# Projections between attention steps, handed out eight products at a time

## The chip, the core and the metric

The kernel runs on one core of a Trainium2 chip. The metric is the device time of one execution in microseconds (us); smaller is better. Five engines work side by side, each through its own queue in order: TensorE (PE in the profile; its weight loads are listed apart as PEld), VectorE (DVE), ScalarE (ACT), GpSimd (POOL) and SyncE (SP), which issues the DMAs. TensorE writes its results into eight PSUM banks of 128 x 512 float32; VectorE and ScalarE read them from there.

## What is computed

One layer of a hybrid decoder, for 1024 tokens of width 1024, in float32:

```python
h = rms_norm(x, g_attn)
z = h @ w_in                       # queries, keys, values, gates of both branches
o_fox = fox_attention(...)         # 8 heads, causal, with a forgetting bias
o_nsa = nsa_attention(...)         # 8 heads, 2 key groups: compressed, selected and window keys
merged = sigmoid(g_a) * (o_fox @ w_br_fox) + sigmoid(g_b) * (o_nsa @ w_br_nsa)
x = x + merged @ w_out
h = rms_norm(x, g_mlp)
x = x + square(relu(h @ w_ff1)) @ w_ff2
return rms_norm(x, g_final)
```

To keep float32 accuracy, an operand is split into an upper part (rounded, "hi") and a lower part (the rest, "lo"), and a product is summed from three combinations: lo x hi, hi x lo and hi x hi.

## The kernel before

The normalised input stays in on-chip memory, transposed and split, as four tiles: `hTh` and `hTl`, one pair for each half of 512 tokens. A **projection** (`proj`) makes 128 output rows for one half: three combinations, each with 8 slices of the inner dimension, are 24 products of 512 columns that add up in one PSUM bank. Its weights are fetched, split by ScalarE (line 206) and VectorE (line 207), and asked for through `wget`. When the last product is issued, `done` takes the bank out and splits the result again.

**Attention** is cut into units: one head and 256 queries in the first stage (FoX), two heads and 256 queries in the second (NSA). A unit has score steps (products of queries and keys; VectorE adds the bias and takes the minimum, line 825; ScalarE takes the exponential, line 838; GpSimd scales, line 841) and then chunks. A **chunk** turns up to four 128 x 128 blocks of the weighted scores (`ptf`, `ptn`: transposes on TensorE, line 160, into one of two PSUM banks of tag "T"), splits the turned tile (`PTf`, `PTn`: a CAST on ScalarE, then a TENSOR_TENSOR on VectorE, both line 864) and multiplies it with the values into `accs`. This is a handover: TensorE to ScalarE to VectorE and back to TensorE. The same two instructions free the T bank, so the transposes of the chunk after next wait for them too.

**What sets the order.** The projections that later units need (and the gates `g`) are written as a list of steps, the feed, each with a cost. `attend` walks through the attention's steps and adds up what the feed is owed by then; when half of the next step's cost is owed, that step is emitted. Attention steps carry a higher priority, and a feed step may not move more than 5000 ns of cost ahead of its place. From this a scheduler with its own time model writes each engine's final instruction order; it may cut a step of several products and put attention instructions between them. Before the change a feed step is four products of one projection: six steps for each half, of `4 * MM` cost.

Not all projections go through the feed: those of the first head pair run before the attention with 256 columns each (`parts=2`). The products of the branches (`brf`, `brn`) have their own steps of six.

The lines that matter: `proj` (316), `wget` (218), `pv` (894: two chunks of transposes run ahead of the first product), `attend` (1114), and the pools with two T banks, three score banks and two projection banks (143 to 154).

Of the kernel before, what the change touches and what calls it, by code (L numbers as in the profile page):

```python
# [120 lines left out]
MM = 216.0  # L121
# [3 lines left out]
class Kernel:  # L125
# [190 lines left out]
    def proj(self, st, n, half, name, done, psf=None, parts=1):  # L316


        nc = self.nc
        box = {}  # L320
        w_ = H // parts

        def part(q, i):
            hi, lo = self.wget(n, name not in self.LATE or half > 0 or i >= 4)
            if q == 0 and i == 0:
                box["ps"] = (psf or self.psP)(f"{name}_{half}")
            c = slice(q * w_, q * w_ + w_)
            hh, hl = self.hT[half]

            ops = ((hi, hh), (hi, hl), (lo, hh)) if parts > 1 else ((lo, hh), (hi, hl), (hi, hh))  # L330
            mm = [(w, h, k) for w, h in ops for k in range(8)]
            for m in range(4 * i, 4 * i + 4):
                w, h, k = mm[m]
                self.mm(box["ps"][:, c], w[:, k, :], h[:, k, c], start=m == 0, stop=m == 23)
            if q == parts - 1 and i == 5:
                done(box["ps"])

        for q in range(parts):
            s = st[q] if parts > 1 else st
            for i in range(6):  # L340
                s.add(4 * MM / parts, lambda q=q, i=i: part(q, i), n)

    def proj_half(self, st, n, half, name, done, psf=None):
        if len(st) == 4:
# [1705 lines left out]
```

## Time and profile before

| | |
|---|---|
| median of 3 runs | 1576.82 us (1576.37 to 1577.49) |
| the profiled execution's own time | 1578.03 us |
| its span, first to last instruction | 1576.3 us |
| instructions | 23267 |
| input and first head pair | 0 to about 100 us |
| FoX units with their feed | about 100 to 345 us |
| NSA units with their feed | about 345 to 830 us |
| merge and MLP | about 830 to 1576 us |

A row of the profile names the source line, engine and operation, then output<-inputs, shapes and a count; behind a bar stand busy time and the mean duration. In a timeline a row begins with its start and length in us, and "[0.72 <-DVE ...]" is the time that the engine stood idle before it and who ended the wait. A row of PEld is a weight load: it runs ahead while the product before it is still flowing, so an idle time shown there is the most that the products themselves can have waited.

### The profile page before, as it was taken

To read this page: it belongs to the slowest core of one execution; us is meant where nothing else is said; L and a number is where in the kernel's file an instruction comes from. 1 tells how busy PE (TensorE), PEld (TensorE's weight loads), DVE (VectorE), ACT (ScalarE), POOL (GpSimd) and SP (SyncE) were. 2 spreads that over 40 slices of the span, in tenths; PEclk is the share of its full clock that TensorE was granted. 3 is DMA by queue.
4 is the path that set the end of the run, shared out by engine and by line. 5 is a ranking of instruction groups with operands and counts; after the bars stand their busy time and mean duration, and the time that the engine had idled before them with its cause. 6 is when DMAs were issued, how large, how long until landed. Compare 5 with 4: busy or idle time off the path is not lost.

```text
span 1576.3 us, 23267 instructions
## 1 busy us (share of the span) xinstructions
PE 1559.3 (99%) x7920; PEld 1314.5 (83%) x7920; DVE 1103.1 (70%) x2450; ACT 861.0 (55%) x1620; POOL 365.5 (23%) x433
## 2 busy tenths in 40 slices
PE   8999999999999999999999999999999999999998
PEld 7888888888888888888888887888888888888886
DVE  7667768757666677648658389665556599777877
ACT  6666666646565676558533267555555644333335
POOL 1133323213333333336310000433333100000002
PEclk9999999999999999999999999999999999999999
DMA  6321211342121112214458542554444696545312
GB/s 192 77 59 49 65 49 56 96 110 65 58 81 57 44 54 74 66 64 135 149 169 314 179 161 87 194 169 155 158 147 147 222 325 215 160 146 167 114 54 107
DMA packets 165951, 196.66 MB, mean 125 GB/s; under 512 B 21497, under 2 KB 101433, under 8 KB 165825
## 3 DMA queue, kind: packets, MB, share of 16 engines
q1 hardware_dynamic: 165832, 195.18, 38.5%
q8 instruction: 63, 1.03, 0.3%
q14 instruction: 56, 0.45, 0.1%
HBM read 139.99 MB, written 55.15 MB: 124 GB/s over the span
## 4 chain that ended last, share of the span: by engine, by line
PE 90%; DVE 4%; DMA 2%; ACT 2%; SPq 1%; issue 1%; POOL 0%; DVEq 0%; ACTq 0%
PE g L157 11%; PE fX L157 11%; PE oX L157 10%; PE accs L157 8%; PE fZ L157 6%; PE oZ L157 5%; PE wo L157 4%; PE ptn L160 3%; PE nq L157 3%; PE brn L157 3%; PE fk L157 3%; PE fv L157 3%; PE fq L157 3%; PE fW L157 2%; PE oW L157 2%; PE sn L157 2%
## 5 line engine op out<-in xcount | busy, mean ns | idle before, releaser
L157 PE MATMUL oX<-to,so 128*128 128x512 f32 x672 | 154.6, 389 | 0.0
L157 PEld LDWEIGHTS oX<-to,so 128*128 128x128 f32 x672 | 126.2, 188 | 26.2
L864 DVE TENSOR_TENSOR PTn<-ptn,PTn 128x512 fp32r<-128x512 f32 (+1 forms) x136 | 90.7, 673 | 70.3 <-ACT PTn L864 69.6
L1873 ACT CAST to<-w 128x1024 fp32r<-128x1024 f32 x48 | 48.2, 1051 | 145.0 <-PE accs L157 54.0
L864 ACT CAST PTn<-ptn 128x512 fp32r<-128x512 f32 (+1 forms) x136 | 76.4, 571 | 64.1 <-PE ptn L160 56.8
L157 PE MATMUL fX<-ht,w1h 128*128 128x512 f32 x384 | 94.9, 389 | 0.6 <-DVE ht L1579 0.6
L1711 POOL TENSOR_TENSOR ss<-w 128x512 f32<-128x512 f32 x14 | 22.4, 1601 | 308.6 <-DMA w<-in_w_ff_dram 188.5
L157 PE MATMUL accs<-PTn,Vnv 128*128 128x512 f32 (+1 forms) x304 | 91.8, 392 | 0.5 <-DVE PTn L864 0.5
L157 PEld LDWEIGHTS fX<-ht,w1h 128*128 128x128 f32 x384 | 72.0, 188 | 15.9 <-DVE ht L1579 1.0
L841 POOL TENSOR_SCALAR pf<-pf,rdf 128x896 f32<-128x896 f32 (+3 forms) x64 | 51.2, 807 | 142.0 <-DVE rdf L840 116.4
L1991 POOL TENSOR_TENSOR z<-x,gf 128x512 f32<-128x512 f32 x8 | 11.0, 1400 | 306.3 <-DVE x L1922 303.9
L157 PE MATMUL oZ<-to,so 128*128 128x512 f32 x336 | 77.6, 389 | 0.0
L157 PE MATMUL g<-hTh,wh_g 128*128 128x512 f32 (+1 forms) x288 | 76.5, 390 | 1.1 <-ACT hTh L311 1.1
L1701 DVE TENSOR_TENSOR w1l<-w,w1h 128x1024 fp32r<-128x1024 f32 (+1 forms) x32 | 34.6, 1081 | 59.7 <-ACT w1h L1700 59.7
L157 PE MATMUL g<-hTl,wh_g 128*128 128x512 f32 (+1 forms) x288 | 75.3, 384 | 0.0
L157 PEld LDWEIGHTS oZ<-to,so 128*128 128x128 f32 x336 | 63.1, 188 | 13.1
L157 PE MATMUL g<-hTh,wl_g 128*128 128x512 f32 x256 | 71.2, 397 | 0.0
L1874 DVE TENSOR_TENSOR so<-hr,so 128x1024 fp32r<-128x1024 f32 x56 | 68.0, 1237 | 1.2 <-ACT so L1873 1.2
L1873 ACT CAST so<-hr 128x1024 fp32r<-128x1024 f32 x56 | 56.7, 1049 | 19.7 <-DMA hr<-hid_d 19.7
L838 ACT ACTIVATE pf<-pf,mf 128x896 f32<-128x896 f32 (+3 forms) x64 | 49.7, 777 | 24.0 <-DVE mf L825 21.5
L1874 DVE TENSOR_TENSOR to<-w,to 128x1024 fp32r<-128x1024 f32 x48 | 56.7, 1221 | 7.7 <-ACT to L1873 7.3
L157 PEld LDWEIGHTS g<-hTh,wh_g 128*128 128x128 f32 x288 | 51.9, 192 | 10.7 <-ACT hTh L311 1.8
(513 smaller groups left out, 4248.7 us busy)
## 6 DMA issues: line engine op xcount, KB each, us to landing
w<-in_w_ff_dram SPq DMA_DIRECT2D x62, 512.0 KB, 4.6
hr<-hid_d SPq DMA_DIRECT2D x56, 512.0 KB, 4.2
wr_wo<-in_w_out_dram SPq DMA_DIRECT2D x20, 512.0 KB, 3.9
x<-in_x_dram SPq DMA_DIRECT2D x16, 512.0 KB, 8.9
wr_g<-in_w_in_dram SPq DMA_DIRECT2D x16, 512.0 KB, 3.8
hid_d<-h22s SPq DMA_DIRECT2D x32, 256.0 KB, 2.1
hid_d<-s2s SPq DMA_DIRECT2D x32, 256.0 KB, 2.0
hid_d<-s3h SPq DMA_DIRECT2D x32, 256.0 KB, 2.3
```

The lines of the kernel that those rows point to most:

```text
L157: self.last = self.nc.tensor.matmul(*a, **k)
L160: self.last = self.nc.tensor.transpose(*a, **k)
L838: nc.scalar.activation(p, p, AF.Exp, bias=nm, scale=-1.0, accum_out=den)
L841: self.scaled = nc.gpsimd.tensor_scalar(p, p, r, 1.0 if gate is None else gate, op0=OP.mult, op1=OP.mult).ins
L864: two = nc.scalar.copy(th, src).ins, nc.vector.tensor_sub(tl, src, th.bitcast(F32)).ins
L1701: nc.vector.tensor_sub(lo, src, hi.bitcast(F32))
L1711: e.tensor_add(p[:, 4:8], b[:, 0:4], b[:, 4:8])
L1873: nc.scalar.copy(o[:, 0, s], src)
L1874: nc.vector.tensor_sub(o[:, 1, s], src, o[:, 0, s].bitcast(F32))
L1991: nc.gpsimd.tensor_mul(y[:, c], x[:, c], gf[:, c])
```

## The change

A feed step of a projection with 512 columns now holds eight products, all of one combination of upper and lower parts, where it held four. There are three such steps for a half, each with twice the cost. Projections with `parts=2` keep steps of four. Nothing else in the program is touched: the same 24 products in the same sequence, the same weights, the same banks.

```diff
@@ proj
         w_ = H // parts
+        size = 4 if parts > 1 else 8
 
         def part(q, i):
-            hi, lo = self.wget(n, name not in self.LATE or half > 0 or i >= 4)
+            hi, lo = self.wget(n, name not in self.LATE or half > 0 or i * size >= 16)
...
             mm = [(w, h, k) for w, h in ops for k in range(8)]
-            for m in range(4 * i, 4 * i + 4):
+            for m in range(size * i, size * i + size):
                 w, h, k = mm[m]
                 self.mm(box["ps"][:, c], w[:, k, :], h[:, k, c], start=m == 0, stop=m == 23)
-            if q == parts - 1 and i == 5:
+            if q == parts - 1 and m == 23:
                 done(box["ps"])
 
         for q in range(parts):
             s = st[q] if parts > 1 else st
-            for i in range(6):
-                s.add(4 * MM / parts, lambda q=q, i=i: part(q, i), n)
+            for i in range(24 // size):
+                s.add(size * MM / parts, lambda q=q, i=i: part(q, i), n)
```

What it does to the order of TensorE is seen at three places. In the rows, `ptf_3_0` is chunk 0 of FoX unit 3, and `ptn_3_8` chunk 8 of NSA unit 3; the last number only makes a name unique.

First place, FoX stage, the keys' compression projection `kc` beside unit 3 of a head (TensorE). Before:

```order
L160 MATMUL ptf_3_0_2890<-idn,pf_7_2829 128x128
L160 MATMUL ptf_3_1_2909<-idn,pf_7_2829 128x128
L160 MATMUL ptf_3_1_2909<-idn,pf_6_2784 128x128
L160 MATMUL ptf_3_1_2909<-idn,pf_7_2829 128x128
L157 MATMUL kc_3113<-hTl_83,wh_kc 128x512 x4
L160 MATMUL ptf_3_2_2917<-idn,pf_6_2784 128x128
L160 MATMUL ptf_3_2_2917<-idn,pf_7_2829 128x128
```

After:

```order
L160 MATMUL ptf_3_0_2890<-idn,pf_7_2829 128x128
L160 MATMUL ptf_3_1_2905<-idn,pf_7_2829 128x128
L160 MATMUL ptf_3_1_2905<-idn,pf_6_2788 128x128
L160 MATMUL ptf_3_1_2905<-idn,pf_7_2829 128x128
L157 MATMUL accs<-PTf_3_2889,Vfv_2130 128x256
L160 MATMUL ptf_3_2_2921<-idn,pf_6_2788 128x128
L157 MATMUL accs<-PTf_3_2889,Vfv_2130 128x256
```

Each piece begins with the last transpose of chunk 0. The four products of `kc` behind the transposes of chunk 1 are gone from here; they follow further down as part of a block of eight. The products with `PTf_3_2889`, the turned tile of chunk 0, now come right behind the transposes; before, `kc` and the transposes of chunk 2 stood ahead of them.

Second place, NSA stage, the second group's values `nv` beside unit 3 (TensorE). Before:

```order
L157 MATMUL accs<-PTn_3_6357,Vnv_4291 128x512 x2
L157 MATMUL nv_1_6506<-hTl_85,wh_nv_6161 128x512 x4
L160 MATMUL ptn_3_9_6453<-idn,wn_6_5927 128x128
L160 MATMUL ptn_3_9_6453<-idn,wn_7_6002 128x128
L160 MATMUL ptn_3_9_6453<-idn,wn_6_6062 128x128
L160 MATMUL ptn_3_9_6453<-idn,wn_7_6124 128x128
L157 MATMUL accs<-PTn_3_6390,Vnv_4291 128x512 x2
L157 MATMUL nv_1_6506<-hTh_84,wh_nv_6161 128x512 x8
L160 MATMUL ptn_3_10_6482<-idn,wn_6_5927 128x128
L160 MATMUL ptn_3_10_6482<-idn,wn_7_6002 128x128
L160 MATMUL ptn_3_10_6482<-idn,wn_6_6062 128x128
L160 MATMUL ptn_3_10_6482<-idn,wn_7_6124 128x128
```

After:

```order
L160 MATMUL ptn_3_8_6424<-idn,wn_6_5927 128x128
L157 MATMUL accs<-PTn_3_6357,Vnv_4291 128x512
L160 MATMUL ptn_3_8_6424<-idn,wn_7_6010 128x128
L160 MATMUL ptn_3_8_6424<-idn,wn_6_6062 128x128
L160 MATMUL ptn_3_8_6424<-idn,wn_7_6124 128x128
L157 MATMUL accs<-PTn_3_6390,Vnv_4291 128x512
L160 MATMUL ptn_3_9_6457<-idn,wn_6_5927 128x128
L160 MATMUL ptn_3_9_6457<-idn,wn_7_6010 128x128
L157 MATMUL accs<-PTn_3_6390,Vnv_4291 128x512
L160 MATMUL ptn_3_9_6457<-idn,wn_6_6062 128x128
L160 MATMUL ptn_3_9_6457<-idn,wn_7_6124 128x128
L160 MATMUL ptn_3_10_6478<-idn,wn_6_5927 128x128
```

Before, blocks of four and eight products of `nv` separate the chunks. Now chunks 8, 9 and 10 stand one behind the other, and the next block of eight comes only after chunk 10.

Third place, NSA stage, the second group's keys `nk` beside unit 1 (TensorE). Before:

```order
L157 MATMUL nk_0_6882<-hTl_83,wh_nk_6613 128x512 x8
L157 MATMUL nk_0_6882<-hTh_82,wh_nk_6613 128x512 x8
L160 MATMUL ptn_1_6_6849<-idn,c_10_6181 128x128
L160 MATMUL ptn_1_6_6849<-idn,c_11_6259 128x128
L157 MATMUL accs<-PTn_1_6743,Vnv_4291 128x512 x2
L157 MATMUL nk_1_7044<-hTh_84,wl_nk_6614 128x512 x4
L157 MATMUL accs<-PTn_1_6807,Vnv_4291 128x512
L160 MATMUL ptn_1_7_6888<-idn,pn_3_6262 128x128
L157 MATMUL accs<-PTn_1_6807,Vnv_4291 128x512
L160 MATMUL ptn_1_7_6888<-idn,pn_3_6417 128x128
L160 MATMUL ptn_1_7_6888<-idn,wn_3_6306 128x128
L160 MATMUL ptn_1_7_6888<-idn,wn_3_6468 128x128
```

After:

```order
L157 MATMUL nk_0_6890<-hTh_82,wh_nk_6619 128x512 x8
L160 MATMUL ptn_1_5_6804<-idn,wn_2_6234 128x128
L160 MATMUL ptn_1_5_6804<-idn,wn_3_6310 128x128
L160 MATMUL ptn_1_5_6804<-idn,wn_2_6383 128x128
L160 MATMUL ptn_1_5_6804<-idn,wn_3_6468 128x128
L157 MATMUL accs<-PTn_1_6695,Vnv_4291 128x512 x2
L160 MATMUL ptn_1_6_6845<-idn,c_10_6181 128x128
L160 MATMUL ptn_1_6_6845<-idn,c_11_6267 128x128
L157 MATMUL accs<-PTn_1_6743,Vnv_4291 128x512 x2
L160 MATMUL ptn_1_7_6877<-idn,pn_3_6270 128x128
L160 MATMUL ptn_1_7_6877<-idn,pn_3_6421 128x128
L160 MATMUL ptn_1_7_6877<-idn,wn_3_6310 128x128
```

Chunk 5 has moved from ahead of `nk_0` (where the first piece does not reach) to behind it, and the four products of `nk_1` between chunks 6 and 7 have gone. On ScalarE the same place reads, before:

```order
L864 CAST PTn_1_6807<-ptn_1_5_6808 128x512
L838 ACTIVATE pn_5_6801,denn_5s<-pn_5_6801,mn_5_12_6820 128x768
L838 ACTIVATE wn_5_6846,denn_5w<-wn_5_6846,mn_5w_6867 128x640
L622 CAST ks_6928<-nk_0_6882 64x512
L623 CAST ks_6928<-nk_0_6882 64x512
L858 CAST PTn_1_6848<-ptn_1_6_6849 64x256
```

and after:

```order
L839 ACTIVATE pn_5_6801,denn_5s<-pn_5_6801,mn_5_12_6824 128x768
L839 ACTIVATE wn_5_6842,denn_5w<-wn_5_6842,mn_5w_6867 128x640
L623 CAST ks_6928<-nk_0_6890 64x512
L624 CAST ks_6928<-nk_0_6890 64x512
L865 CAST PTn_1_6803<-ptn_1_5_6804 128x512
L859 CAST PTn_1_6844<-ptn_1_6_6845 64x256
```

The cast of chunk 5's tile (`ptn_1_5`) stood ahead of the two casts of `nk_0`; now it stands behind them.

## The prediction

> **What bounds the kernel now.** I read the page's busy times first, then the chain of waits, then the busy times by stage, and last the list of who waits for whom, on TensorE's two rows, in the two attention stages that the change touches.
>
> ```profile
> span 1576.3 us, 23267 instructions
> ...
> PE 1559.3 (99%) x7920; PEld 1314.5 (83%) x7920; DVE 1103.1 (70%) x2450; ACT 861.0 (55%) x1620; POOL 365.5 (23%) x433
> ...
> PE 90%; DVE 4%; DMA 2%; ACT 2%; SPq 1%; issue 1%; POOL 0%; DVEq 0%; ACTq 0%
> ```
>
> TensorE is busy all the time and makes 90% of the chain that ended last. A change can win only by taking away waits of TensorE, and lose only by adding them. How many there are in the touched stages:
>
> ```profile
> core 0: us, PE busy (x) PEld busy (x) DVE busy (x) ACT busy (x) POOL busy (x), PEclk, DMA share, GB/s
> 0.00:100.00 100.00, 94.21 (x626) 82.71 (x627) 71.56 (x184) 65.88 (x126) 20.77 (x39) 0.98 0.45 122
> 100.00:345.00 245.00, 244.40 (x1452) 213.53 (x1451) 175.46 (x494) 148.67 (x304) 72.74 (x84) 1.00 0.24 68
> 345.00:830.00 485.00, 482.94 (x2556) 408.22 (x2555) 316.60 (x1089) 291.04 (x696) 169.39 (x246) 1.00 0.27 84
> ```
>
> Products stand still for 0.6 us in the FoX stage and 2.1 us in the NSA stage, but a product's shown end includes its way through the array, so short waits hide in it. The weight loads show more. FoX stage first, then NSA stage, with the sum, the number and the longest wait:
>
> ```profile
> PEld ptf L160 <- DVE PTf L864: 1.8, 4, 0.6
> ...
> PEld accs L157 <- DVE PTf L864: 0.4, 1, 0.4
> ...
> PEld accs L157 <- DVE PTn L864: 1.2, 3, 0.7
> PEld accs L157 <- DVE PTn L859: 1.1, 2, 0.9
> PEld sn L157 <- DVE mn L825: 0.8, 1, 0.8
> PEld ptn L160 <- DVE PTn L864: 0.6, 2, 0.4
> PEld sn_2w L157 <- DVE mn L825: 0.5, 1, 0.5
> ```
>
> With the small ones left out here (1.7 us in FoX, 1.0 us in NSA) these waits are 9.1 us in 730 us. That is the ceiling of any gain. Of these, 4.0 us (1.8 + 0.4 + 1.2 + 0.6) are at the handover of line 864: transposes, CAST, TENSOR_TENSOR, and then either the products with the turned tile or the next transposes into the same bank. So the question is what the new order does to these handovers.
>
> **The price of a handover and of what stands in it.** The place of `kc` in the old order shows one in full (timeline); the rows behind it, from the chain of waits, the timeline and the costliest groups, price the instructions of TensorE:
>
> ```profile
> 241.92 0.66 PE L160 MATMUL ptf<-idn,pf 128*128 128x128 f32 x4 [0.21 <-DVE PTf L864]
> ...
> 242.66 0.59 ACT L864 CAST PTf<-ptf 128x512 fp32r<-128x512 f32 x1 [1.04 <-PE ptf L160]
> ...
> 243.28 0.69 DVE L864 TENSOR_TENSOR PTf<-ptf,PTf 128x512 fp32r<-128x512 f32 x1 [0.83 <-ACT PTf L864]
> ...
> 244.03 0.19 PEld L157 LDWEIGHTS accs<-PTf,Vfv 128*128 128x128 f32 x1 [0.38 <-DVE PTf L864]
> ...
> 992.40 5.44 PE fX L157 x24
> ...
> 106.95 1.20 PE L157 MATMUL accs<-PTf,Vfv 128*128 128x256 f32 x8
> ...
> 533.58 0.60 PE L160 MATMUL ptn<-idn,wn 128*128 128x128 f32 x4
> ...
> L157 PE MATMUL oX<-to,so 128*128 128x512 f32 x672 | 154.6, 389 | 0.0
> ...
> 243.46 0.27 PE L160 MATMUL ptf<-idn,pf 128*128 128x128 f32 x1
> ...
> 243.49 0.36 PE L157 MATMUL accs<-PTf,Vfv 128*128 128x256 f32 x1
> ```
>
> The last of four transposes starts 0.27 us before their end at 242.58, at 242.31; the first product with the tile starts at 244.03. The handover costs 1.72 us from the start of the last transpose, with neither engine held up by other work. What TensorE issues in between covers it: a product of 512 columns takes 0.227 us (5.44 / 24), one of 256 columns 0.12 us ((1.20 - 0.36) / 7), a transpose 0.11 us ((0.60 - 0.27) / 3). The old order at this place has one transpose of chunk 0, three of chunk 1 and four products of `kc` before the bank is wanted again: 0.11 + 0.33 + 0.91 = 1.35 us, so 0.37 us of wait, and the row of the products shows 0.38. The price fits.
>
> **The change part by part.** The work is the same: 35 projections of two halves and 24 products, 1680 products in 210 steps instead of 420. No product, transpose, cast or DMA is added; I cost the work itself at nothing. What moves is where the products stand. In TensorE's order the rows of four products of these projections fall from 139 to 35, and those of eight rise from 72 to 108. A block of four covers 0.91 us of a handover and needs 0.8 us of other work beside it; a block of eight covers 1.82 us, more than it needs, but leaves the next gap empty. I went through the new order chunk by chunk, took the spacing from the last transpose to whoever needs the tile or its bank, and set it against 1.72 us:
>
> - `kc`, the first place: the products with `PTf_3_2889` come 0.11 + 0.33 = 0.44 us after the transpose, a wait of 1.28. The two waits of 0.37 there before are covered by it. **+0.54**.
> - The same unit one and two heads earlier (beside `fk`): one transpose, eight products of 256 and three transposes, 0.11 + 0.96 + 0.33 = 1.40, wait 0.32, twice. There was a block of four there before, and no wait. **+0.64**.
> - `nv`, the second place: chunk 6 has a spacing of 1.44 (wait 0.28); then chunk 10's transposes need the bank of chunk 8 with one transpose, two products of 512 and four transposes in between, 0.11 + 0.45 + 0.44 = 1.00 (wait 0.72). **+1.00**.
> - Beside gate 6 (`g_6`), chunk 5 after chunk 3: 0.11 + 0.23 + 0.45 + 0.44 = 1.23, wait 0.49. **+0.49**.
> - Beside gate 5 in the third pair, chunk 9 after chunk 7, again 1.00. **+0.72**.
>
> The third place, `nk`, needs ScalarE's queue. Before:
>
> ```profile
> 565.91 1.98 PE L157 MATMUL nk<-hTh,wh_nk 128*128 128x512 f32 x8
> ...
> 567.92 0.58 ACT L622 CAST ks<-nk 64x512 fp32r<-64x512 f32 x1 [0.84 <-PE nk L157]
> ...
> 568.52 0.58 ACT L623 CAST ks<-nk 64x512 fp32r<-64x512 f32 x1
> ...
> 569.13 0.68 DVE L624 TENSOR_TENSOR ks<-nk,ks 64x512 fp32r<-64x512 f32 x1 [1.78 <-ACT ks L623]
> ...
> 572.26 0.19 PEld L157 LDWEIGHTS accs<-PTn,vcmp 128*128 128x128 f32 x1 [0.92 <-DVE PTn L859]
> ```
>
> Now the cast of chunk 5 is queued behind the two casts of `nk_0`, and its subtraction behind that of `nk_0` on VectorE. From the end of `nk_0`'s last product the tile is ready after 0.03 + 1.18 + 0.03 + 0.68 + 0.69, about 2.6 us (two casts, then the two subtractions one after the other). TensorE wants chunk 5's bank for chunk 7 about 1.4 us after that end: ten instructions of 1.57 us, less the last product's way out of 0.16 us (0.389 - 0.227). The wait is about 1.2 us; the 0.92 us in the row above, 4 us further on, then falls away, as everything behind it is later. **+0.28**. If it stays, the place costs 0.9 more.
>
> One place gets better, beside the branch of FoX:
>
> ```profile
> 740.60 0.30 PEld L157 LDWEIGHTS sn_2w<-kw,Qnq 128*128 128x128 f32 x2 [0.49 <-DVE mn L825]
> ...
> 741.27 0.30 PEld L157 LDWEIGHTS sn<-ks,Qnq 128*128 128x128 f32 x2 [0.37 <-DVE mn_3w L825]
> ...
> 742.29 0.19 PEld L157 LDWEIGHTS accs<-PTn,Vnv 128*128 128x128 f32 x1 [0.72 <-DVE PTn L864]
> ```
>
> The two transposes that end chunk 0 have moved 0.68 us forward, so about 0.6 of the last wait goes; the scores moved back by 0.22 wait that much longer for VectorE. **-0.40**.
>
> The sum is 0.54 + 0.64 + 1.00 + 0.49 + 0.72 + 0.28 - 0.40 = 3.3 us, each place at the price of a handover with free queues. They are not always free. At `nv` the new order has a weight split directly ahead of chunk 6's cast, on both engines:
>
> ```profile
> L206 ACT CAST wh_g<-wr_g 128x1024 fp32r<-128x1024 f32 x16 | 16.7, 1042 | 0.0
> ...
> L207 DVE TENSOR_TENSOR wl_g<-wr_g,wh_g 128x1024 fp32r<-128x1024 f32 x16 | 19.9, 1243 | 4.6 <-ACT wh_g L206 4.4
> ```
>
> It is an instruction of 1.04 and 1.24 us, and a handover that comes during it waits half of one on average. I add 0.5 us for that, bounded by nothing below and by the longest wait of the old order, 0.92 us, at each of the seven places above, 6.4 us. So +3.8 us: 1581.8 for an execution like the profiled one (1578.0), and, as that one lies 1.2 us above the median of the runs shown (1576.8), **1580.6 us** against that median.
>
> **The rivals.**
>
> *The waits trade places, no change.* The 9.1 us hold some 5 us beside those counted above, and a TensorE that is held up at one place finds later tiles ready. If the new waits use up the old ones nearby, as at `nk`, the sum is about 0 and the time 1576.8. Speaking for it is the `nk` place. Against it, the other places that get worse have no old wait close behind.
>
> *Eight cover a handover, faster.* 1.82 us is more than 1.72, and 0.91 is not. Were there a block in each handover, the 4.0 us on line 864 would go: 1572.8. Against it stand the three places in the order, where the block comes once in two or three chunks. It decides the sign if the new order's handovers without a block are fewer than the old ones with half of one; I count more. [...] The trace shows no gain from longer batches alone: the eight of `nk` above take (1.98 - 0.389) / 7, again 0.227 us each.
>
> *The queues behind, much slower.* Chunks that come without projection work between them, one in 0.89 us (four transposes and two products), ask ScalarE for 0.59 and VectorE for 0.69 each time, on top of softmax and splits; VectorE is busy for 316.6 of 485 us in the NSA stage. If each of the seven places met a queue as long as the longest wait before, 6.4 us come on top: 1576.8 + 3.3 + 6.4 = 1586.5.
>
> *The clock drops.* More waits could cost TensorE its clock: 0.98 stands in the first 100 us, which hold its long waits, and 1.00 in both attention stages with 9.1 us of short ones. A loss of 0.02 in one stretch of 245 us is 4.9 us: with the sum 1585.5. [...]
>
> *The change does nothing,* because the scheduler cuts the steps again. It does cut some (64 rows of one product), but the counts of fours and eights show that most blocks stand.
>
> **How the numbers follow.** More handovers uncovered, +2 to +6 us: 56%. Traded, within 2 us: 22%. Queues, +6 to +12: 12%. Eight cover, -2 to -5: 7%. Clock: 3%. A measurement of this kernel can tell about 0.2%, 3.2 us, from no change. The forecast lies just above that, so a quarter of the first case counts as no change: slower 0.42 + 0.12 + 0.03 = 0.57; faster only where the fourth case goes beyond 3.2 us or so, 0.06; no change the rest, 0.37. The range for 8 in 10 runs from the traded case, 1576.6, to the queues' 1586.5; the forecast alone holds 1579 to 1583.
>
> **What would show it.** In the profile after: waits of PEld on line 864 (there line 865) of about 7 us in the two stages instead of 4.0, with one of 1.2 us or more at `kc` (near 241 us) and one at `nk` (near 568 us), and clocks of 1.00. The branches, merge and MLP behind 830 us should be the same but shifted. Wrong would be: these sums at 4 or less, or a loss that stands in other rows, such as weights' DMAs or scores.

## The result, and the profile after

The changed kernel takes 1588.09 us (median of 5 executions, 1587.08 to 1588.99) against 1576.72 us in the same session: a ratio of 1.0067, with a 95% interval of 1.0057 to 1.0078. It is **slower by 11.4 us (0.7%)** by the medians, 10.6 by the ratio. The prediction had the sign; the size is three times the 3.8 us that it gave, and lies above its range (1586.5).

The page of the profiled execution (1588.99 us), and TensorE by stage (start and end of the stretch, its length, then busy time and number of instructions of each engine, granted clock, DMA):

```profile
span 1587.3 us, 23244 instructions
...
PE 1563.8 (99%) x7920; PEld 1314.6 (83%) x7920; DVE 1104.3 (70%) x2450; ACT 861.7 (54%) x1620; POOL 363.0 (23%) x433
...
PE 91%; DVE 4%; ACT 2%; DMA 2%; issue 1%; SPq 1%; DVEq 0%; ACTq 0%
```

```profile
100.00:345.00 245.00, 240.13 (x1413) 209.03 (x1411) 171.55 (x492) 148.98 (x302) 71.79 (x81) 0.99 0.24 68
345.00:830.00 485.00, 479.45 (x2534) 403.66 (x2534) 316.87 (x1084) 288.72 (x691) 168.47 (x250) 1.00 0.27 82
```

The span grew by 11.0 us; PE stands still for 4.9 us of the FoX stretch (0.6 before) and 5.6 us of the NSA stretch (2.1 before), and in the FoX stage the clock is no longer 1.00. Who waits for whom, for weight loads, first from 100 to 345 us, then from 345 to 841 us (sum, number, longest):

```profile
PEld accs L157 <- DVE PTf L865: 2.3, 4, 1.4
PEld hT_kc L160 <- ACT PTf L865: 1.4, 1, 1.4
PEld hT_vc L160 <- DVE sg_vc L716: 1.3, 1, 1.3
...
PEld nq L157 <- DVE wl_nq L207: 0.9, 1, 0.9
```

```profile
PEld ptn L160 <- DVE PTn L865: 4.1, 4, 1.9
PEld accs L157 <- DVE PTn L865: 3.4, 6, 1.5
PEld sn L157 <- DVE mn L826: 0.8, 1, 0.8
PEld sn_2w L157 <- DVE mn L826: 0.7, 1, 0.7
```

The handover of line 864 (now 865) has 9.8 us of waits (2.3 + 4.1 + 3.4) instead of 4.0. Three rows are new in kind: `hT_kc`, `hT_vc` and `nq`. They belong to the compression of the keys and values, whose last steps (a sigmoid, two transposes `hT`) stand beside the end of the FoX stage, and to the first projection of the NSA stage.

For a finer account I took, for every instruction of TensorE, the time from its start to the next start, less the lower quartile of the same sequence of shapes (the instruction before, itself and the next) in the kernel before. From 100 to 840 us these **excess times** are 5.4 us (FoX) and 10.7 us (NSA) before, and 12.1 and 15.9 us after: 11.8 us more. The changed kernel leaves these stages 11.8 us later than the kernel before, and 0.9 of that is given back behind them, which leaves the 11.0 of the span. All figures called excess below are made so; products at a slow clock count in them. Behind 840 us the work is the same.

Two places show the kind of loss. The first lies between the two attention stages. Rows of the changed kernel's timeline, then of the kernel before at the same place:

```profile
322.81 1.22 DVE L207 TENSOR_TENSOR wl_w1vc<-wr_w1vc,wh_w1vc 128x1024 fp32r<-128x1024 f32 x1
...
324.05 0.37 SPq L187 DMA_DIRECT2D wr_nk<-in_w_in_dram  x1
...
330.51 1.05 ACT L206 CAST wh_nk<-wr_nk 128x1024 fp32r<-128x1024 f32 x1 [2.73 <-DMA wr_nk<-in_w_in_dram]
...
333.54 0.43 PE L160 MATMUL hT_vc<-idn,sg_vc 126*128 126x126 f32 x2 [1.06 <-DVE sg_vc L716]
...
334.67 3.53 PE L157 MATMUL nq<-hTh,wl_nq 128*128 128x512 f32 x8 [0.70 <-DVE wl_nq L207]
...
337.99 2.20 PE L157 MATMUL nq<-hTl,wh_nq 128*128 128x512 f32 x8
```

```profile
318.50 0.99 SPq L187 DMA_DIRECT2D wr_nk<-in_w_in_dram  x2
...
323.34 1.05 ACT L206 CAST wh_nk<-wr_nk 128x1024 fp32r<-128x1024 f32 x1 [0.46 <-DMA wr_nk<-in_w_in_dram]
...
329.71 2.11 PE L157 MATMUL nq<-hTh,wl_nq 128*128 128x512 f32 x8
```

Weights are loaded into two buffers. The DMA for `nk` goes out when the split of the compression's third weight tile has freed its buffer, at 324.05 instead of 318.50 us. ScalarE then stands 2.73 us for it with the sigmoid of `sg_vc` and the cast of `nq` queued behind, VectorE's instructions follow, and TensorE waits at `hT_vc` and at `nq`. Before, the same products started without a wait. Behind these waits eight products of `nq` take 3.32 us (334.67 to 337.99), 0.415 us each instead of 0.227. The stretches of the changed kernel around it:

```profile
332.00:335.00 3.00, 1.25 (x8) 0.74 (x7) 2.97 (x6) 2.40 (x4) 1.32 (x1) 1.00 0.32 67
335.00:339.00 4.00, 4.00 (x12) 3.14 (x11) 1.77 (x4) 1.04 (x1) 0.09 (x1) 0.58 1.14 281
```

The granted clock is 0.58 over 4 us, that is 1.7 us lost (0.42 x 4).

The second place is chunk 6 beside `nv`, for which the prediction had a wait of 0.28:

```profile
541.48 0.59 ACT L647 COPY vtnv<-nv 128x512 f32<-128x512 f32 x1 [3.00 <-PE nv L157]
...
541.96 1.05 ACT L206 CAST wh_nq<-wr_nq 128x1024 fp32r<-128x1024 f32 x1
...
542.90 1.07 ACT L865 CAST PTn<-ptn 128x512 fp32r<-128x512 f32 x2
...
543.04 1.22 DVE L207 TENSOR_TENSOR wl_nq<-wr_nq,wh_nq 128x1024 fp32r<-128x1024 f32 x1 [3.84 <-ACT wh_nq L206]
...
544.18 1.28 DVE L865 TENSOR_TENSOR PTn<-ptn,PTn 128x512 fp32r<-128x512 f32 x2
...
544.92 0.50 PE L157 MATMUL accs<-PTn,Vnv 128*128 128x512 f32 x1 [1.28 <-DVE PTn L865]
```

The copy out of `nv` and a weight split, both called up by the end of `nv`, stand directly ahead of the chunk's CAST and TENSOR_TENSOR, and no products of the feed are left to cover them. The excess is 1.53 us. In the kernel before, the copy and the split stand ahead of a chunk's CAST too, but blocks of four products of `nq` (the one shown and one at 540.67 us) lie between, and no product waits for the turned tile:

```profile
538.89 1.05 ACT L206 CAST wh_nq<-wr_nq 128x1024 fp32r<-128x1024 f32 x1
539.06 1.09 PE L157 MATMUL nq<-hTh,wl_nq 128*128 128x512 f32 x4
...
539.84 0.59 ACT L864 CAST PTn<-ptn 128x512 fp32r<-128x512 f32 x1
```

### The profile page after: what moved, and what is told of

It is laid out like the page before. It is cut to its first block, busy times and chain, and to the rows that moved or that the text cites. A ratio compares the mean times of both kernels' runs of the same rounds, so it can differ in the third digit from the quotient of the medians.

```text
span 1587.3 us, 23244 instructions
## 1 busy us (share of the span) xinstructions
PE 1563.8 (99%) x7920; PEld 1314.6 (83%) x7920; DVE 1104.3 (70%) x2450; ACT 861.7 (54%) x1620; POOL 363.0 (23%) x433
## 4 chain that ended last, share of the span: by engine, by line
PE 91%; DVE 4%; ACT 2%; DMA 2%; issue 1%; SPq 1%; DVEq 0%; ACTq 0%
PE fX L157 11%; PE g L157 10%; PE oX L157 10%; PE accs L157 8%; PE fZ L157 5%; PE wo L157 5%; PE oZ L157 5%; PE ptn L160 3%; PE nq L157 3%; PE brn L157 3%; PE fq L157 2%; PE fv L157 2%; PE fW L157 2%; PE brf L157 2%; PE oW L157 2%; PE fk L157 2%
## 5 line engine op out<-in xcount | busy, mean ns | idle before, releaser
L157 PE MATMUL accs<-PTn,Vnv 128*128 128x512 f32 (+1 forms) x304 | 97.1, 400 | 1.8 <-DVE PTn L865 1.7
L1712 POOL TENSOR_TENSOR ss<-w 128x512 f32<-128x512 f32 x14 | 22.4, 1603 | 307.8 <-DMA w<-in_w_ff_dram 188.0
L157 PEld LDWEIGHTS fX<-ht,w1h 128*128 128x128 f32 x384 | 72.0, 188 | 15.9 <-DVE ht L1580 1.0
L839 ACT ACTIVATE pn<-pn,mn 128x128 f32<-128x128 f32 (+3 forms) x64 | 49.6, 775 | 34.3 <-DVE mn L826 32.8
```

Source lines behind the costliest of these rows:

```text
L157: self.last = self.nc.tensor.matmul(*a, **k)
L839: nc.scalar.activation(p, p, AF.Exp, bias=nm, scale=-1.0, accum_out=den)
L1712: e.tensor_add(p[:, 4:8], b[:, 0:4], b[:, 4:8])
```

## The experiments

The theory after the result (A): coarse steps push what hangs on a projection's end or start (copies, weight splits, the freeing of weight buffers, the compression's steps) together into places where no products are left. The rival that the prediction stood on (B): the loss is handovers without cover, whatever the queues. Times are differences from the kernel before, from the ratio of that session, with its interval.

**The change in halves.** `FOX` and `G01` name what is fed beside the FoX units: `fk`, `fq` and `fv` (keys, queries and values of later FoX heads), `kc` and `vc` (the compression's keys and values), and the first two gates.

```diff
-        size = 4 if parts > 1 else 8
+        size = 8 if parts == 1 and (name[:2] in self.FOX or name in self.G01) else 4
```

and, in the second run, the other way round:

```diff
-        size = 4 if parts > 1 else 8
+        size = 4 if parts > 1 or name[:2] in self.FOX or name in self.G01 else 8
```

> Steps of eight only for the projections that are fed beside the FoX units (fk, fq, fv, kc, vc and the first two gates); the NSA stage's projections stay at four. The changed kernel is 11.4 us slower than the one before. Theory A (weights late): the trace of the changed kernel puts 7.3 us of the loss ahead of 345 us, 3.8 of it at one place near 335 us where the casts of the weights of nk and nq wait for their DMAs and the TensorE clock then falls; so this kernel should take 1576.7 + 7.3 = 1584.0. Theory B (the sum of the prediction scaled up: uncovered handovers, each with a queue ahead): 1.2 of the 3.3 us lay in this stage, so 1576.7 + 4.1 = 1580.9. In both a clock of 0.99 from 100 to 345 us only if the place near 335 us is kept.

> The other half of the change: steps of eight only for the NSA stage's projections, four beside the FoX units. Theory A: the trace of the changed kernel adds 4.6 us between 345 and 840 us and gives 0.7 back behind it, so 1576.7 + 3.9 = 1580.6. Theory B: 2.1 of the 3.3 us, scaled, so 1576.7 + 7.3 = 1584.0. If the two halves do not act on each other, this one and the FoX half add up to the 11.4 us of the whole change within 1 us.

Measured: +4.9 us (3.3 to 6.5) and +5.2 us (3.2 to 7.1). Together 10.1, which is the whole within the intervals: that the stages act on each other is not seen. Excess in the FoX stage 10.7 us with the first, in the NSA stage 16.1 us with the second, the other stage as before in both. Neither theory's split was right in time: FoX's share lies between the two. The 4.9 us mix two groups of executions of the first kernel, four of 1580.6 to 1580.9 us and four of 1583 to 1585 us with a lower mean clock (0.997 and 0.998 instead of 0.999). In its profiled execution (1580.9) the two waits were there, but the slow clock was not:

```profile
332.86 0.43 PE L160 MATMUL hT_vc<-idn,sg_vc 126*128 126x126 f32 x2 [0.92 <-DVE sg_vc L716]
333.99 2.12 PE L157 MATMUL nq<-hTh,wl_nq 128*128 128x512 f32 x8 [0.69 <-DVE wl_nq L207]
...
335.00:339.00 4.00, 4.00 (x22) 3.37 (x21) 1.55 (x2) 1.05 (x1) 0.00 (x0) 1.00 0.94 241
```

(two rows of its timeline and one stretch). The clock can hold through nearly the same waits.

**The gates between the compression's steps back to four.**

```diff
-        size = 4 if parts > 1 else 8
+        size = 4 if parts > 1 or name in self.G01 else 8
```

> The changed kernel, but the two gates that are fed between the compression's own steps (g_0 behind kc, g_1 behind vc) go back to four. Theory A: a block of compression steps is placed by a count of the feed's cost; with steps of 1728 instead of 864 the first of them comes one step behind the blocks it reads instead of three, and the turn behind the last step of the gate instead of ahead of it; the weight splits are pushed together there. Undoing it should take the waits at hT_kc (1.4 us) and at hT_vc and nq with the slow clock (3.8 us) away: 1588.1 - 5.2 = 1582.9, clock 1.00. Theory B: only handovers count, and the two gates hold none of the seven places that were counted: within 1 us of 1588.1.

Measured: +8.8 us (6.8 to 10.7), 1.8 less than the 10.6 of the whole change by its ratio, which the intervals do not hold apart; A wanted 5.2 less, B none. The waits at `hT_kc` and `hT_vc` and the slow clock are gone (FoX excess 9.0 instead of 12.1), `nq` still waits 0.5, and three new waits of 0.2 to 0.6 came at 273, 300 and 330 us. Undoing the part next to a wait moves some of it.

**The weights of `nk` in a buffer of their own.**

```diff
-        self.early = {n: lambda: (self.att, "Q", 4) for n in ("fq0", "fv0")}
+        self.early = {n: lambda: (self.att, "Q", 4) for n in ("fq0", "fv0", "nk0")}
```

> The changed kernel with one weight tile, nk's, loaded into a buffer of its own (a free query buffer), so that its DMA need not wait until the split of the compression's third weight tile has freed one of the two load buffers; nq's load then moves one buffer forward too. TensorE's, VectorE's and ScalarE's orders stay the same up to this place. Theory A: the cast of nk no longer waits 2.73 us for its DMA, the waits of 1.1 us (hT_vc) and 0.9 us (nq) near 334 us go, and with them the half clock behind them (1.9 us): 1588.1 - 3.8 = 1584.3, clock 1.00 from 335 to 339 us. Theory B: the waits there stem from the order of the engines, not from the load: 1588.1 within 0.7, the half clock stays. A third reading, that the slow clock has nothing to do with the waits: they go (-1.9) but the slow products stay: 1586.2.

Timeline rows and the stretch of the slow clock:

```profile
327.58 1.05 ACT L206 CAST wh_nk<-wr_nk 128x1024 fp32r<-128x1024 f32 x1
...
332.14 0.38 PE L160 MATMUL hT_vc<-idn,sg_vc 126*128 126x126 f32 x2
332.28 2.08 PE L157 MATMUL nq<-hTh,wl_nq 128*128 128x512 f32 x8
...
335.00:339.00 4.00, 4.00 (x21) 3.33 (x20) 0.23 (x1) 0.00 (x0) 0.00 (x0) 1.00 0.90 228
```

The cast no longer waits, both waits and the slow clock are gone, and the FoX excess falls from 12.1 to 8.2 us: the 3.8 that A named, with the engines' orders unchanged up to this place. So the late buffer is shown as the cause of the waits at `hT_vc` and `nq`; the 1.13 us at `hT_kc` stayed. The time says less: +9.8 us (7.7 to 12.0), not told apart from 10.6. In the NSA stage 1.0 us of excess came back, half of it at the first products of `nv` (0.48 at 357 us).

**The size of the step.** `size = 12`, 6, 3 and 2 in place of 8.

> Feed steps of twelve products instead of eight (two for a half). Theory A (coarse steps leave longer stretches of attention without a product to cover a handover, and push what a projection's end and the next weights need into one place): the loss grows with the step, eight cost 11.4 us over four, so twelve cost some 20: 1597 (1590 to 1604). Theory C (each size has its own luck with the scheduler's order): anywhere from 1577 to 1600, not above eight by rule.

> Feed steps of six products. Theory A: between four and eight, 1576.7 + 5.7 = 1582.4 (1579 to 1586). Theory C: as likely outside these bounds as inside. Six products cover 1.36 us, less than a handover of 1.72, so by the rival of the prediction that wants a block longer than a handover, six would be no better than four.

> Feed steps of three products, the other way. Theory A: finer steps spread the cover more evenly, so it is at least as good as four: 1573 to 1577. Theory C: anything from 1573 to 1582. The 16 us of waits that TensorE has with four bound the gain.

> Feed steps of two products. Theory A: as with three or a little better, 1572 to 1577, with less than 16 us of waits of TensorE in the attention stages. Theory C: anything from 1573 to 1582.

| products in a step | 12 | 8 | 6 | 4 | 3 | 2 |
|---|---|---|---|---|---|---|
| time against four, us | +19.7 | +10.6 | +1.4 | 0 | +0.5 | +4.1 |
| interval | 17.0 to 22.4 | 9.0 to 12.3 | -0.2 to 2.8 | | -1.1 to 1.9 | 2.5 to 5.8 |
| excess FoX / NSA, us | 10.2 / 28.0 | 12.1 / 15.9 | 8.4 / 10.6 | 5.4 / 10.7 | 6.7 / 10.3 | 10.9 / 9.7 |

Above six the loss grows steeply, twelve as A said. Six misses A's 5.7, and finer steps win nothing: A's half of the table towards small steps is wrong. Theory C, luck with the order, is not excluded there: the places of these four kernels were not followed one by one. In the NSA stage six, four, three and two are within 1 us of each other; in the FoX stage every other size is worse than four. Twelve shows the slow clock again, twice, near 611 and near 755 us. The first time it comes behind a wait of 2.8 us, with next to no DMA traffic in its second part (one row of the timeline, then stretches):

```profile
610.95 1.42 PE L157 MATMUL sn<-ks,Qnq 128*128 128x384 f32 x4 [2.78 <-DVE mn L826]
...
608.00:611.00 3.00, 0.22 (x3) 0.05 (x1) 2.91 (x9) 1.85 (x7) 0.32 (x1) 1.00 0.03 5
611.00:613.00 2.00, 2.00 (x9) 1.79 (x9) 1.94 (x6) 1.07 (x2) 0.07 (x1) 0.59 0.95 253
613.00:615.00 2.00, 2.00 (x8) 1.57 (x7) 1.98 (x9) 1.68 (x5) 1.09 (x1) 0.56 0.02 6
```

**One weight split off the queue.** The kernel with eight in the NSA stage, and:

```diff
+            if name == "nq3":
+                nc.gpsimd.tensor_scalar(hi, raw, 1.0, 1.0, op0=OP.mult, op1=OP.mult)
+                nc.gpsimd.tensor_sub(lo, raw, hi.bitcast(F32))
+            else:
                 nc.scalar.copy(hi, raw)
                 nc.vector.tensor_sub(lo, raw, hi.bitcast(F32))
```

> Eight in the NSA stage only, as in the second experiment, with one weight split, that of nq for the fourth head pair, done by GpSimd instead of ScalarE and VectorE. TensorE's order stays the same word for word. Theory A: the wait of 1.53 us at chunk 6 beside nv is the split's (1.05 us on ScalarE, 1.22 on VectorE, directly ahead of the chunk's CAST and TENSOR_TENSOR); with the split gone the prediction's own figure for this place, 0.28, or less should show, and the waits of TensorE in the NSA stage fall from 16.1 to about 14.8 us; time 1.3 us below the second experiment, 3.9 above the kernel before. Theory B: the wait is the price of the handover without cover: it stays at 1.5.

The same chunk, timeline:

```profile
535.93 0.59 ACT L651 COPY vtnv<-nv 128x512 f32<-128x512 f32 x1 [3.00 <-PE nv L157]
536.84 0.59 ACT L869 CAST PTn<-ptn 128x512 fp32r<-128x512 f32 x1 [0.32 <-PE ptn L160]
...
537.46 0.69 DVE L869 TENSOR_TENSOR PTn<-ptn,PTn 128x512 fp32r<-128x512 f32 x1 [3.81 <-ACT PTn L869]
...
538.20 0.50 PE L157 MATMUL accs<-PTn,Vnv 128*128 128x512 f32 x1
```

The excess falls from 1.53 to 0.36 us, with TensorE's order the same. The prediction's 0.28 was the price with free queues, and the split is the other 1.2. In time nothing can be told: +4.6 us (2.7 to 6.5) against +5.2; the NSA excess fell by 0.5 only (16.1 to 15.6), as the wait at `nk` is 1.63 here and 1.27 in the second experiment. TensorE's order is the same in both; what makes it the one or the other is not shown.

**FoX at eight, `nk` early; four and three; `kc` back to four.** The first has both edits shown above; the second is the second run's line with 3 for 8; the third adds `name != "kc"` to the first run's line.

> Eight beside the FoX units only, as in the first experiment, with nk's weights loaded into a buffer of their own, as in the fourth. The first experiment had executions of 1580.7 and of 1583 to 1585, the long ones with a lower mean clock; its profiled execution waited 1.0 and 0.9 us at hT_vc and nq without losing the clock, that of the changed kernel waited 1.1 and 0.9 and lost it. Theory A (the two waits put the clock at risk): without the waits no execution is much above the others, and the median lies at 1577.5 + 4.9 - 1.9 - 1 = 1579.5, at most 1581 for the longest. Rival: the scatter has nothing to do with this place and stays, with the longest 3 to 4 us above the shortest.

> A version that may beat both kernels: four beside the FoX units, three in the NSA stage. By the trace the waits of TensorE are 5.4 us with four, 6.7 with three and 10.9 with two in the FoX stage, and 10.7, 9.3 and 9.7 us in the NSA stage. If the stages add up, 1.4 us is won: 0.1%, 1575.7 against 1577.1, which the interval can hardly tell from no change. If they do not, 1576 to 1580.

> Eight beside the FoX units only, except kc, which goes back to four. By the sum of the prediction kc's place costs 0.54 net (1.28 less two old waits of 0.37), measured 1.37 less 0.72; so 0.65 us should come back, with 1.37 near 242 us gone and 0.38 and 0.34 back. Rival: where kc's steps stand also decides how the compression's steps behind it fall, so more than this comes back or other waits appear: the waits at 267 and 290 us (0.64 together) would change too.

With `nk` early FoX at eight costs +2.2 us (0.8 to 3.6) instead of 4.9; excess in the FoX stage 8.4 instead of 10.7, and 0.8 more in the NSA stage. The longest execution lies above A's 1581 (1581.8) and 3.3 us above the shortest, as the rival said. But executions of the kernel before lie up to 4 us apart too: whether the scatter of the first experiment came from the clock at this place stays open. Four and three: +0.2 us (-1.3 to 1.6), no gain. The 9.3 us of excess in its expectation left out one wait of 0.97 us at a pair of shapes that the kernel before does not have; with it, it is 10.3.

`kc` at four: +0.9 us (-0.5 to 2.4), where 0.65 less than 4.9, that is 4.2, was expected. The rival holds: `hT_kc`, `hT_vc` and `nq` no longer wait. But the 1.37 us at `kc` itself stayed, so the prediction's reason for it, a block that became one of eight, cannot be the whole of it. Hence the counterpart, with `FOX = "kc", "vc"` in the first run's line (fk, fq, fv at four):

> Eight only for kc, vc and the two gates between them; the FoX units' own projections fk, fq, fv and the whole NSA stage at four. With kc alone at four the wait of 1.37 us at 242 us stayed, so it is not kc's block of eight by itself. Theory D (the phase: how much the feed is behind when unit 3 turns its chunks, which the earlier steps set): with the earlier steps at four the old order at kc comes back, 0.38 and 0.34 there instead of 1.37; the waits at hT_kc, hT_vc and nq (2 to 3 us) stay, since the delays of the compression's steps are counted in kc's and the gates' own steps. Time 1577.0 + 3 = 1580. Rival: kc's block of eight is enough for the 1.37, which would mean that either alone, kc or the ones ahead of it, makes it.

Measured: -0.2 us (-1.4 to 1.3). At `kc`, timeline of this one, then of the one with `kc` at four:

```profile
241.44 0.66 PE L160 MATMUL ptf<-idn,pf 128*128 128x128 f32 x4 [1.13 <-DVE PTf L865]
```

```profile
243.10 0.39 PE L157 MATMUL accs<-PTf,Vfv 128*128 128x256 f32 x1 [1.13 <-DVE PTf L865]
```

Theory D falls twice. The wait at `kc` is there with either part at eight (excess 1.29 and 1.37). And the waits at `hT_kc`, `hT_vc` and `nq` go when `kc` alone is at four, and also when `fk`, `fq` and `fv` are; a smaller one of 0.59 us stands at the first product of `vc`, behind `hT_kc`. These two kernels cost 0.9 and -0.2 us, the one with all at eight 4.9. So the waits do not belong to one step. That they are a coincidence of phases, how far the feed has come when the attention's last units turn their chunks, is argued from these runs and not shown.

**Two causes undone in the changed kernel:** `kc` at four and that split on GpSimd.

> The changed kernel with two causes undone: kc at four, and the split of nq for the fourth pair on GpSimd. TensorE's order is that of the kc experiment up to the NSA stage and that of the NSA experiment in it. If the causes found are separate and their sizes are right, the waits of TensorE are 7.6 us in the FoX stage and 15.6 in the NSA stage (10.9 and 15.7 in the changed kernel, but one of these is a wait of 0.3 to 0.4 more at nk and at 752 us in some executions), no slow clock near 335 us, and the time lies 6 to 7 us above the kernel before instead of 11.4. If it lies within 1.5 us of the changed kernel, the sizes were read from the trace wrongly.

Measured: +4.9 us (2.8 to 6.8), 1 to 2 us below the expectation; excess 7.7 and 15.2 us against 7.6 and 15.6 expected; clock 1.00 from 335 to 339 us. About half of the loss is taken back (5.7 of 10.6 us, each known to some 2 us), most of it by `kc` at four (4.4 us of excess in the FoX stage, 0.7 in the NSA stage), which works by the order behind it and not for the reason that the prediction gave.

## Why the prediction was right and wrong

**Right: what bounds the kernel, and the sign.** The loss is waits of TensorE in the two attention stages, nothing of it lies behind 840 us, and "eight cover a handover" did not come: a block of eight comes once in two or three chunks, and the chunks between are bare.

**The seven places, in excess over the old waits there:**

| place | predicted, us | measured, us |
|---|---|---|
| beside `fk`, twice | +0.64 | +0.67 |
| `kc` | +0.54 | +0.66 (1.37 less 0.38 and 0.34) |
| `g_6` | +0.49 | +0.49 |
| gate 5 | +0.72 | +0.67 |
| `nv`, chunks 6 and 10 | +1.00 | +2.18 (1.53 and 0.66) |
| `nk` | +0.28 | +0.72 (1.63 less 0.91) |
| near 742 us | -0.40 | +0.36 (1.48 less 1.12) |
| sum | 3.3 | 5.7 |

The price of a handover, 1.72 us less what stands in it, holds to 0.1 us where the queues are free (the first four rows). At `kc` the spacing was read rightly from the new order, but the block of eight alone does not explain it: the same 1.37 us stands there with `kc` at four. At `nk` the profiles of the second, third and fourth experiments have 1.27, 1.27 and 1.28 us instead of 1.63, close to the 1.2 of the prediction.

**Two steps failed. One is the queue term**, "I add 0.5 us for that", an average for one place; the seven places took 2.4 us more than their price with free queues. At `nv` the prediction saw the split directly ahead of the chunk's cast and took half of one. But the order is fixed, so the chunk does not meet the split by chance: the wait is 1.53 us in the changed kernel and in the second, third and fourth experiments alike, and 1.2 us of it is the split, shown by moving it. For the other places, `nk` excepted, the prediction does not say what stands ahead on ScalarE and VectorE. Near 742 us it is a split too, on VectorE ahead of the minima that free the scores' banks:

```profile
748.02 1.56 DVE L207 TENSOR_TENSOR wl_brf<-wr_brf,wh_brf 128x1024 fp32r<-128x1024 f32 x1
...
749.50 0.47 DVE L826 CUSTOM_DVE_ANT_0 pn<-sn,ww,mn 128x256 f32<-128x256 f32 x1
...
752.51 0.62 PE L157 MATMUL sn_2w<-kw,Qnq 128*128 128x384 f32 x2 [0.33 <-DVE mn L826]
```

That this split makes the whole difference there is argued from the rows; it was not moved alone.

**The other step, and the larger, is the list of places, which was too short:** 4.9 us of new waits lie outside it, and the slow clock behind two of them. I went through the handovers of line 864 and left out what else TensorE takes from other engines. `hT_kc` (1.13), `hT_vc` (1.14) and `nq` (0.92) are 3.2 us, and smaller new waits near 188, 268, 290 and 613 us another 1.7. The sentence that "a loss that stands in other rows, such as weights' DMAs" would prove the prediction wrong is what happened: `nk`'s DMA was late, which makes the waits at `hT_vc` and `nq`. What makes the one at `hT_kc` stays open; it goes with `kc`, with the FoX projections or with the two gates at four. I had costed weights at nothing because none was added; that a split sets when a load buffer comes free, and that splits move with the steps, was the missing line.

**Traded waits: a little.** Old waits of 1.7 us near 143, 178, 269, 273, 542, 587 and 809 us are gone. I had allowed the 0.92 at `nk`, which went as said.

**The clock.** The rival had 3%: before, the clock was 1.00 in both attention stages, with 9.1 us of short waits. Behind two waits of 1.1 and 0.9 us close together the clock was 0.50 for 3.41 us of the profiled execution, a loss of 1.7 us.

With these, 5.7 + 4.9 + 1.7 - 1.7 = 10.6 of the 11.8 us of excess stand by name; the rest is in waits under 0.15 us. Of the signposts, waits of about 7 us at the handover were 9.8, kc (1.4) and nk (1.6) came at their places, and the clock of 1.00 did not hold. The range failed because its upper end took the queue at seven places as the worst case and let no term stand for places not counted.

## What to carry to other kernels

When a change only reorders work, read the new order on every engine at each place, not on the bound engine alone: what stands ahead of the instruction that TensorE will wait for prices the wait, and in this kernel it was a weight split of 1.05 and 1.22 us. Follow each buffer that is freed by a moved instruction to the DMA that waits for it. And when a handover model finds several small losses of one sign and few gains, leave room above the sum for places that the model does not list.

## What the runs showed of the hardware

In the traces of the two kernels TensorE's granted clock is 1.00 or 0.50. In the attention stages of the changed kernel one stretch has 0.50, 3.41 us long, so it costs 1.7 us. With steps of twelve two have: the second is 3.41 us long too, the first, near 611 us, lost 1.7 us by its two stretches in the experiments (0.41 x 2 + 0.44 x 2). A slow stretch with the one before it, first in the changed kernel, then the second one of twelve, and last the same place in the first experiment, which kept the clock through nearly the same waits (1.0 and 0.9 us):

```profile
331.57:334.98 3.41, 1.66 (x11) 1.17 (x11) 3.35 (x5) 2.67 (x5) 1.30 (x1) 1.00 0.28 57
334.98:338.40 3.42, 3.42 (x9) 2.63 (x8) 1.19 (x4) 1.04 (x1) 0.11 (x1) 0.50 1.16 288
...
751.30:754.71 3.41, 2.24 (x11) 1.14 (x9) 3.35 (x12) 2.80 (x8) 0.00 (x0) 1.00 0.66 211
754.71:758.12 3.41, 3.41 (x13) 3.28 (x14) 2.69 (x14) 2.12 (x5) 2.32 (x3) 0.50 0.42 138
...
330.45:333.86 3.41, 1.93 (x15) 1.45 (x14) 2.91 (x5) 3.11 (x6) 0.88 (x1) 1.00 0.15 29
333.86:337.27 3.41, 3.29 (x14) 2.74 (x15) 1.46 (x4) 0.85 (x1) 0.55 (x1) 1.00 1.13 272
```

The first two pairs are cut where the clock changes; in the first experiment, where it stays at 1.00, they are two stretches of the same length. In the changed kernel TensorE was busy for 1.66 of the 3.41 us ahead of the slow stretch and with twelve for 2.24 us; in the first experiment it was busy for 1.93 us of the first of the two, and the clock held. So how long TensorE was busy in these stretches does not by itself tell whether the clock falls. Why nearly the same waits went with a slow clock in one execution and not in another is not shown.
